# A decoder step of four recurrent branches: tile order, two groups of products on another engine, and re-timed side steps

## The chip, the cores and the metric

The kernel runs on one core of a Trainium2 chip. The metric is the time of one execution on the device in microseconds (us). A core has five engines that run side by side: PE (TensorE, matrix products), DVE (VectorE) and ACT (ScalarE) for elementwise work, POOL (GpSimd), and SP (SyncE), which here only issues DMA transfers.

## The reference

One layer of a hybrid recurrent decoder, on 2,096 positions (32 sample tokens of 8 sequences, 16 meta tokens, 2,048 prompt tokens), width 1,024:

```
u = x @ w_in                      # all branches' columns at once
A: xbc = silu(causal_conv(xbc));  chunked Mamba-2 scan, per-head RMS norm, * silu(z_a)
B: S5: diagonal complex state space, 16 groups of 16 channels, 64 states each;
   lb = exp(lam*dt), powers of lb, gelu, gated by a sigmoid product,       * silu(z_b)
C: qkv = silu(causal_conv(qkv)); q, k = l2norm(q), l2norm(k); gated DeltaNet in chunks:
   a triangular inverse per chunk, then a scan over chunks, RMS norm,      * silu(z_c)
D: HGRN2: f = lower bound + sigmoid, k = 1 - f; sum over q*k*decay, scan,  * silu(z_d)
out = concat(A, B, C, D) @ w_out
x   = layernorm(alpha * x + out)
```

The outputs are x and the seven final states, for the prompt and for each sample sequence.

## The kernel before, in words

After the input layer norm (phase1a), the positions are done in two halves (1,072 and 1,024). In each half `proj` (L585) runs 22 tiles of the input projection: one tile is 128 output columns times the half's positions, in 3 blocks (half 0: 384, 304, 384 columns) or 2 (half 1: 512), each of 24 matmuls into the PSUM tile pj. w and x are split in a high and a low part, hence three products of 8 each. After a block its `use` runs: for a tile with convolution (letters k, l, v, x in ORDER, L52) ScalarE copies pj to raw (L630 to L637), GpSimd makes cv = raw * w3 + b (L641), VectorE adds three shifted products (L643), ScalarE applies silu (L649 to L654), and SyncE stores it (L656: x to xbc_d, v to qkv_d); k and l then pass an l2 norm (`l2n`, L664). For f the `use` is two sigmoids and two scalings (L828 to L833); a, b, c, d are the gates z with silu (L815), q is D's query. The strings ORDER[0] and ORDER[1] give the order of the 22 tiles.

Everything else is "side work": Python generators ("jobs") that are resumed between the projection's matmuls. A job's `yield d` means: go on after d us of a clock that sums the nominal cost of the matmuls written so far (`_pe`, L115; `poll`, L140). Where the program needs a job to be finished, `drain` (L160) steps that clock on without projection matmuls between. TensorE runs its instructions in exactly the order in which the program was written so; the other engines' order comes from a scheduler. A changed number in a `yield` therefore moves that job's matmuls a few places along TensorE's order, and the scheduler's other queues follow.

The jobs that the change touches, and the names of their tiles:

- `small_loads` (L222): parameters, transposed on TensorE. `gates` (L484): A's and C's decays; te (L548) and g_rw (L565) come from cumulative sums, g_rw is transposed on TensorE and stored to rows_d.
- `b_setup` (L893): B's tables. `rot` (L977) builds cosT and sinT by doubling in rounds of products (L960 to L965, L999, L1000). L1061 and L1062 are 16 + 16 products of 128x144 into Pw and tw9, L1065 adds them (128x2304). L1074 to L1076 make four bs_wt, each transposed on TensorE. `b_main`, `b_tail`: B's scans.
- `c_pre` (L732): C's decay matrices; cdec is loaded from rows_d, masked on GpSimd (L727), exponentiated on ScalarE (L729), and multiplied into cma (L753, L755). `base_inv` (L763) inverts the small triangular blocks (acc) step by step on VectorE, `c_inv` and `c_chunk` use them.
- `d_group` (L1580): D. d_pr is the query-key product (L1596, buffers d_pra and d_prb), reduced per head by hsel on TensorE; Q blocks Qa, Qb (L1600) and running decays d_tota, d_totb follow on VectorE.
- At the first block of the tile with index LAST (L53), `last()` waits for the inverses, gives back the memory of the half, and in half 0 begins the next half's phase1a, in half 1 starts the heads of C and A (`c_head`, L1493) and their chunks. In the last stage, `out_chunk` (L1831) makes the 17 output chunks.

## Time and profile before

| what | value |
|---|---|
| three executions | 1395.56, 1398.35, 1405.71 us; median 1398.35 |
| the profiled execution | 1396.38 us, its span 1394.6 us, mean granted clock 0.945 |
| TensorE, matrix products | 1278.1 us busy, 92% |
| TensorE, weight loads | 1078.6 us, 77% |
| VectorE | 908.5 us, 65% |
| ScalarE | 573.4 us, 41% |
| GpSimd | 434.3 us, 31% |

The span runs from the first to the last instruction that the profiler recorded. The share of busy time is a mean over stages with different limits. An engine's idle time is put down to what released it ("releaser"). The granted clock is TensorE's, as a share of its full 2.4 GHz. In a row of the timeline stand the start in us, the duration in us, engine, line, operation, output and inputs, and in brackets the idle time before it with its releaser.

### The profile page before, as it was taken

The page shows a single profiled execution, that of the slowest core. Times are in us where ns is not written, and L with a number is a line of the kernel's source. Part 1 is how long each engine was busy: PE and PEld are TensorE (multiplying, and loading weights), DVE is VectorE, ACT ScalarE, POOL GpSimd, SP SyncE. Part 2 cuts the span into 40 slices and gives each one's busy share as a digit, 9 for nine tenths or more (in the row PEclk, how much of TensorE's full clock was granted, in tenths as well). Part 3 has the DMA queues.
Part 4 walks back from the last instruction along what each step waited for, and adds up shares of the span by engine and source line. Part 5 has one row for each costly group of instructions (what it writes and reads, how often), then busy time and mean ns, then how long its engine had stood idle before and what let it go on. Part 6 is the DMA issues. An engine that isn't in the chain of part 4 may idle for free.

```text
span 1394.6 us, 23821 instructions
## 1 busy us (share of the span) xinstructions
PE 1278.1 (92%) x8596; PEld 1078.6 (77%) x8596; DVE 908.5 (65%) x2269; ACT 573.4 (41%) x1089; POOL 434.3 (31%) x403
## 2 busy tenths in 40 slices
PE   6985996888999999999989889999997999999997
PEld 5885896877879998987767678778675677777886
DVE  8799623764698747766437598963347566756654
ACT  3234436366523443436375455353334333333211
POOL 4135111321211100102112222120115576677665
PEclk9998999998989999999999989999998999999999
DMA  8521243346424825313642734135639876776343
GB/s 220 175 84 42 55 149 91 90 133 196 127 76 143 236 77 189 110 46 96 184 135 72 249 112 118 51 105 147 173 99 284 202 216 188 204 191 201 118 121 107
DMA packets 259007, 195.80 MB, mean 140 GB/s; under 512 B 70949, under 2 KB 231927, under 8 KB 258872
## 3 DMA queue, kind: packets, MB, share of 16 engines
q1 hardware_dynamic: 258890, 194.28, 48.8%
q8 instruction: 68, 1.11, 0.4%
q14 instruction: 49, 0.40, 0.1%
HBM read 125.01 MB, written 64.31 MB: 136 GB/s over the span
## 4 chain that ended last, share of the span: by engine, by line
PE 49%; DVE 19%; DMA 14%; ACT 6%; POOL 5%; issue 4%; SPq 2%; POOLq 0%; DVEq 0%; ACTq 0%
PE pj L128 30%; PE pq L128 16%; DMA cdec<-rows_d 3%; PE pq L122 3%; DVE cv L643 2%; DMA f_R<-r_d 2%; DMA b<-b 1%; DMA bc<-nrm 1%; DVE w L582 1%; DMA a_L<-rows_d 1%; DVE Qa L1671 1%; DMA wr<-in_w_in_dram 1%; POOL xt L1870 1%; POOL xt L1871 1%; DVE d_ATa L1675 1%
## 5 line engine op out<-in xcount | busy, mean ns | idle before, releaser
L128 PE MATMUL pj<-xh,w 128*128 128x384 f32 (+2 forms) x1760 | 540.6, 375 | 7.9 <-ACT zs L832 3.1
L128 PEld LDWEIGHTS pj<-xh,w 128*128 128x128 f32 x1760 | 335.4, 197 | 52.9 <-issue 10.6
L128 PE MATMUL pj<-xl,w 128*128 128x384 f32 (+2 forms) x880 | 320.2, 364 | 0.0
L128 PEld LDWEIGHTS pj<-xl,w 128*128 128x128 f32 x880 | 174.2, 198 | 12.0 <-issue 0.2
L641 POOL TENSOR_SCALAR cv<-raw,par 128x384 f32<-128x384 f32 (+2 forms) x50 | 52.0, 1041 | 233.8 <-ACT raw L637 189.2
L128 PE MATMUL pj<-woh,o_mh 128*128 128x512 f32 (+2 forms) x280 | 116.1, 415 | 0.0
L128 PE MATMUL pj<-woh,o_ml 128*128 128x512 f32 (+2 forms) x280 | 109.0, 389 | 0.0
L128 PE MATMUL pj<-wol,o_mh 128*128 128x512 f32 (+2 forms) x280 | 108.9, 389 | 0.0
L643 DVE SCALAR_TENSOR_TENSOR cv<-raw,par,cv 128x384 f32<-128x384 f32 (+2 forms) x150 | 102.2, 683 | 9.7 <-POOL cv L641 8.8
L128 PE MATMUL pj<-w,xh 128*128 128x256 f32 (+3 forms) x544 | 105.9, 295 | 0.3 <-ACT xh L90 0.2
L128 PEld LDWEIGHTS pj<-w,xh 128*128 128x128 f32 (+1 forms) x544 | 85.1, 190 | 1.7 <-ACT xh L90 1.2
L128 PE MATMUL pj<-w,xl 128*128 128x256 f32 (+3 forms) x272 | 78.2, 291 | 1.5 <-DVE xl L90 1.5
L582 DVE TENSOR_TENSOR w<-wr,w 128x1024 fp32r<-128x1024 f32 x44 | 55.3, 1256 | 31.4 <-ACT w L581 31.3
L727 POOL TENSOR_TENSOR cdec<-cdec,negm 128x256 f32<-128x256 f32 x32 | 25.3, 791 | 159.1 <-DMA cdec<-rows_d 139.5
L128 PEld LDWEIGHTS pj<-woh,o_ml 128*128 128x128 f32 (+1 forms) x280 | 52.1, 186 | 12.7 <-issue 0.9
L128 PEld LDWEIGHTS pj<-woh,o_mh 128*128 128x128 f32 (+1 forms) x280 | 52.2, 187 | 10.9 <-issue 0.7
L128 PEld LDWEIGHTS pj<-wol,o_mh 128*128 128x128 f32 (+1 forms) x280 | 52.3, 187 | 8.2 <-issue 0.2
L310 POOL TENSOR_TENSOR lnrs<-lnve,mhalf 128x1 f32<-128x1 f32 (+1 forms) x34 | 23.9, 704 | 105.8 <-DVE lnve L90 60.9
L753 DVE SCALAR_TENSOR_TENSOR cma<-pq,nbeta,cdec 128x128 f32<-128x128 f32 (+1 forms) x68 | 23.0, 339 | 49.0 <-ACT cdec L729 33.1
L128 PEld LDWEIGHTS pj<-w,xl 128*128 128x128 f32 (+1 forms) x272 | 51.4, 191 | 2.0 <-DVE xl L90 1.9
L581 ACT CAST w<-wr 128x1024 fp32r<-128x1024 f32 x44 | 46.0, 1046 | 16.7 <-DMA wr<-in_w_in_dram 11.9
L1773 POOL TENSOR_TENSOR f_r<-f_r,mhalf 128x12 f32<-128x12 f32 x17 | 38.8, 2283 | 29.7 <-DVE f_r L1772 29.7
(570 smaller groups left out, 2574.8 us busy)
## 6 DMA issues: line engine op xcount, KB each, us to landing
wr<-in_w_in_dram SPq DMA_DIRECT2D x46, 512.0 KB
xt<-in_x_prompt_dram SPq DMA_DIRECT2D x16, 512.0 KB
xn_d<-xt SPq DMA_DIRECT2D x16, 512.0 KB
ma<-cma SPq DMA_DIRECT2D x64, 128.0 KB
xt<-xn_d SPq DMA_DIRECT2D x16, 512.0 KB
out_dram<-xt SPq DMA_DIRECT2D x15, 512.0 KB
f_R<-r_d SPq DMA_DIRECT2D x32, 192.0 KB
cdec<-rows_d SPq DMA_DIRECT2D x32, 128.0 KB
```

Source lines behind the costliest of these rows:

```text
L122: self._pe(self.PE.transpose(out, in_, self.ident[r, r]), 0.02 + n / 1200)
L128: self._pe(self.PE.matmul(out, lhsT, rhs, start=start, stop=stop, **kw), 0.01 + n * (1 if rhs.dtype == F32R else 4) / 2400)
L310: self.G.tensor_tensor(rs[:n], ve[:n], self.mhalf[:n, 0:1], ALU.pow)
L581: S.copy(w[:, :, 0], raw)
L582: V.tensor_tensor(w[:, :, 1], raw, w[:, :, 0].bitcast(F32), SUB)
L641: G.tensor_scalar(cv[:, 0:m], raw[:, 3:3 + m], w[3], b, op0=MUL, op1=ADD)
L643: V.scalar_tensor_tensor(cv[:, 0:m], raw[:, k:k + m], w[k], cv[:, 0:m], op0=MUL, op1=ADD)
L727: G.tensor_tensor(d[:n, :, :n], d[:n, :, :n], m[:n, None, :n].to_broadcast([n, nh, n]), ADD)
L753: V.scalar_tensor_tensor(ma[:n, 0, h, :n], pks[h][:n, 0, :n], self.nbeta[:n, t, 2 * p + h:2 * p + h + 1], dec[:n, h, :n], op0=MUL, op1=MUL)
L1671: V.tensor_tensor(qv, qv, tv[r, :, :, 0:1].to_broadcast([64, 2, nbt, s]), MUL)
L1675: V.copy_predicated(AV[:nn, :, :, 1, :], mk, pa[:nn])
L1773: G.tensor_tensor(r, r, self.mhalf[:, 0:12], ALU.pow)
```

## The change

ORDER[0] goes from "qkkqbbllxvffvxxxccadda" to "qkkqbbllxffvvxcxxcadad", ORDER[1] from "kkbbqqllffvvxxxxccadda" to "kkbbqqllffvxxaxvxccadd", and LAST from 17 and 17 to 21 and 17. The products of L1061 and L1062, the sum of L1065 and the product of L1596 move from GpSimd to VectorE. Some twenty `yield` numbers change. The number of matmuls stays. VectorE has 42 instructions more (33 of the set-up, 9 of L1596), GpSimd 42 fewer; ScalarE's table loads go from 84 to 74, by the order in which its activations stand. The diff, with one line of surroundings:

```diff
@@ -49,8 +49,8 @@
 KORD = [0, 1, 4, 5, 6, 7, 2, 3]
-ORDER = ["qkkqbbllxvffvxxxccadda", "kkbbqqllffvvxxxxccadda"]
-LAST = [17, 17]
+ORDER = ["qkkqbbllxffvvxcxxcadad", "kkbbqqllffvxxaxvxccadd"]
+LAST = [21, 17]
 HEAD = META + NS
@@ -222,7 +222,7 @@
         a, V = self.a, self.Vp
-        yield 2.3
+        yield 3.6
 
@@ -240,7 +240,7 @@
                 yield 4.2
-        yield 3.8
+        yield 2.9
         p = self.pt()
@@ -530,7 +530,7 @@
 
-        yield 19.0
+        yield 19.0 if o else 24.7
         pa = self.pt()
@@ -555,7 +555,7 @@
                             self.segmask[:, :, None].to_broadcast([48, NSEG, 8]), MUL)
-            yield 1.0
+            yield 0.0
             pc = self.pt()
@@ -566,7 +566,7 @@
             k = min(8, N - t0)
-            yield 2.1
+            yield 2.7 if o else 2.1
             pt = self.pt()
@@ -685,7 +685,7 @@
                                 op=ADD, axis=mybir.AxisListType.X)
-        yield 9.0 if half else 6.1
+        yield 9.0 if half else 7.2
         p = self.pt()
@@ -697,7 +697,7 @@
             V.tensor_scalar(rf, rf, scale, None, op0=MUL)
-        yield 4.5 if half else 7.8
+        yield 4.5 if half else 6.4
         pt = self.pt()
@@ -789,7 +789,7 @@
                 V.tensor_tensor(T[:npar, j + 1:B, 0:j + 1], T[:npar, j + 1:B, 0:j + 1], tv, ADD)
-                yield 0.0 + m * (j + 1) / 240
+                yield 0.4 + m * (j + 1) / 240
             G.tensor_copy(D[:npar], T[:npar].rearrange("p i c -> p c i"))
@@ -921,7 +921,7 @@
         self.exp_acc(tp, mag, lrd)
-        yield 2.3
+        yield 2.7
         V.tensor_tensor(ang, li, dt, MUL)
@@ -946,7 +946,7 @@
         S.activation(cs, r2, AF.Sin)
-        yield 0.7
+        yield 0.6
 
@@ -987,7 +987,7 @@
             while w <= 64:
-                yield 1.6
+                yield 1.9
                 for c in range(0, min(w, 65 - w), 16):
@@ -1023,7 +1023,7 @@
         V.tensor_tensor(ci, ci, den, MUL)
-        yield 2.1
+        yield 0.9
         V.tensor_scalar(b2[0:64], b2[0:64], -1.0, None, op0=MUL)
@@ -1044,7 +1044,7 @@
                 self.ld(cl[:, :, j], a[nm][0].rearrange("(h g) q n -> (g q) h n", h=2))
-            yield 1.0
+            yield 0.9
             p = self.pt()
@@ -1058,11 +1058,11 @@
             yb = Yc[:, g:g + 1, :].to_broadcast(s9)
-            G.tensor_tensor(self.Pw[:, g], xb, pr[:, :, g:g + 1].to_broadcast(s9), MUL)
-            G.tensor_tensor(tw9[:, g], yb, pi[:, :, g:g + 1].to_broadcast(s9), MUL)
+            V.tensor_tensor(self.Pw[:, g], xb, pr[:, :, g:g + 1].to_broadcast(s9), MUL)
+            V.tensor_tensor(tw9[:, g], yb, pi[:, :, g:g + 1].to_broadcast(s9), MUL)
             if g % 4 == 3:
                 yield 2.5
-        G.tensor_tensor(self.Pw, self.Pw, tw9, ADD)
+        V.tensor_tensor(self.Pw, self.Pw, tw9, ADD)
 
@@ -1125,7 +1125,7 @@
         for hq in range(2):
-            yield 0.9 if hq else 4.7
+            yield 1.2 if hq else 4.7
             p = self.pt()
@@ -1133,7 +1133,7 @@
         for gh in range(2):
-            yield 1.0 if gh else 2.0
+            yield 1.0 if gh else 2.4 if blk < 2 else 2.0
             p = self.pt()
@@ -1172,7 +1172,7 @@
                          p.rearrange("p (g i q) -> p g i q", g=4, i=8), AF.Gelu_apprx_tanh)
-            yield 3.5 if hq else 3.9
+            yield 3.0 if hq else 3.9
         y5 = tp.tile([128, 2, 64, 8], F32, name="b2")
@@ -1215,7 +1215,7 @@
         S.copy(U, p[:, 0:288].rearrange("p (g c) -> p g c", g=16))
-        yield 5.0
+        yield 4.4
         p = self.pt()
@@ -1263,7 +1263,7 @@
                          p[:10].rearrange("p (g i q) -> p g i q", g=4, i=8), AF.Gelu_apprx_tanh)
-            yield 2.6
+            yield 2.8
         yield 1.7
@@ -1390,7 +1390,7 @@
                         dap(self.tb_d, (((NT + t0 + c) * 4) * 4 + b) * 1024, [[32, 32], [4096, 4], [1, 32]]))
-        yield 27.2 if t0 == 1 else 8.0
+        yield 28.0 if t0 == 1 else 8.0
         kd, vb = [], []
@@ -1508,7 +1508,7 @@
         qe, ke = eqk[:, 0], eqk[:, 1]
-        yield 10.8
+        yield 10.0
         p = self.pt()
@@ -1593,12 +1593,12 @@
         pr = tp.tile([128, 2, 256], F32, name="d_pr" + sfx)
-        G.tensor_tensor(pr[:, :, :NTK], qf[:, 0:2, :NTK], kS[:, :, :NTK], MUL)
+        V.tensor_tensor(pr[:, :, :NTK], qf[:, 0:2, :NTK], kS[:, :, :NTK], MUL)
         Q = self.Qbd[sfx]
         for h in range(2):
             r = slice(64 * h, 64 * h + 64)
             V.tensor_tensor(Q[r, :, h, :NTK], qf[r, 0:2, :NTK], qf[r, 2:4, :NTK], MUL)
-        yield 13.6 if tail else 8.0
+        yield 13.6 if tail else 7.0 if t0c in (1, 9, 11) else 8.0
         p = self.pt()
@@ -1760,7 +1760,7 @@
                         axis=mybir.AxisListType.X)
-        yield 1.1
+        yield 1.3
         p = self.pt()
@@ -1825,7 +1825,7 @@
                 self.bo = self.bcast_row(op2, a["ln_b"], "o_bo")
-            yield 8.9
+            yield 10.6 if half else 6.8
             self.done.add(("wo", half))
```

How instructions move is shown at three places.

VectorE, from the tile te on (half 0, tile 1; te is what the transposed g_rw waits beside; cv is the convolution, bs_wt the first of three set-up tables that TensorE transposes behind it). Before:

```order
L548 TENSOR_TENSOR te<-g_tot,g_acum 128x72
L962 TENSOR_TENSOR bvr<-bvr,bm_1369 128x16
L643 SCALAR_TENSOR_TENSOR cv<-raw,par,cv 128x384
L964 TENSOR_TENSOR bs_l<-sinT,bur 128x256
L1074 TENSOR_TENSOR bs_wt<-bs_X,bpr 128x128 x4
L643 SCALAR_TENSOR_TENSOR cv<-raw,par,cv 128x328
L964 TENSOR_TENSOR bm_1369<-bui,bur 128x16
L552 TENSOR_TENSOR dtte<-sp_115,te 128x36
L573 COPY g_rs<-pq 128x128
L643 SCALAR_TENSOR_TENSOR cv<-raw,par,cv 128x384
L965 TENSOR_TENSOR sinT<-sinT,bs_l 128x16x16
L660 COPY cprev<-raw 128x3
```

and now:

```order
L548 TENSOR_TENSOR te<-g_tot,g_acum 128x72
L1000 COPY bui<-bvi 128x16
L960 TENSOR_TENSOR cosT<-cosT,bur 128x16x16
L960 TENSOR_TENSOR bvr<-bur 128x16
L961 TENSOR_TENSOR bs_l<-sinT,bui 128x256
L963 TENSOR_TENSOR sinT<-cosT,bui 128x16x16
L961 TENSOR_TENSOR bm_1362<-bui 128x16
L963 TENSOR_TENSOR bvi<-bur,bui 128x16
L552 TENSOR_TENSOR dtte<-sp_115,te 128x36
L962 TENSOR_TENSOR cosT<-cosT,bs_l 128x16x16
L1074 TENSOR_TENSOR bs_wt<-bs_X,bpr 128x128 x4
L962 TENSOR_TENSOR bvr<-bvr,bm_1362 128x16
```

Before, the addition L1076 into bs_wt is the next row, behind three convolution rows; now two rows of the rotation (L960 to L965) follow, then L1076, and no convolution row stands between.

ScalarE, in half 0 around tiles 10 to 12 (zs is f's sigmoid, cdec C's decay, ACT_TABLE_LOAD the switch between their tables). Before:

```order
L828 ACT_TABLE_LOAD
L828 ACTIVATE zs<-pj 128x384
L832 ACTIVATE zs<-pj 128x384
L829 ACTIVATE zs<-zs,lb,lb_606 128x384
L833 ACTIVATE zs<-zs,lb_606 128x384
L729 ACT_TABLE_LOAD
L729 ACTIVATE cdec<-cdec,nac 128x128 x4
L828 ACT_TABLE_LOAD
L828 ACTIVATE zs<-pj 128x384
L832 ACTIVATE zs<-pj 128x384
L581 CAST w_3553<-wr 128x8x128
L829 ACTIVATE zs<-zs,lb,lb_606 128x384
```

and now:

```order
L828 ACTIVATE zs<-pj 128x304
L832 ACTIVATE zs<-pj 128x304
L829 ACTIVATE zs<-zs,lb,lb_616 128x304
L833 ACTIVATE zs<-zs,lb_616 128x304
L729 ACT_TABLE_LOAD
L729 ACTIVATE cdec<-cdec,nac 128x128 x2
L1140 COPY b_3378<-pq 128x512
L729 ACTIVATE cdec<-cdec,nac 128x128 x2
L1140 COPY b_3378<-pq 128x512
L729 ACTIVATE cdec<-cdec,nac 128x128 x4
L828 ACT_TABLE_LOAD
L828 ACTIVATE zs<-pj 128x384
```

Before, sigmoid and decay alternate with a load each time; now the blocks of f above the first shown row share one load with it, and eight decay activations stand in one row before the next switch.

SyncE, in half 1 from the last convolved tile's stores on (xbc_d and qkv_d hold convolved x and v; c_qk, c_aq, ep and c_N are what `c_head` reads). Before:

```order
L1709 DMA od_d<-d_oya 128x2x128
L656 DMA xbc_d<-zs 128x512
L796 DMA tb_d<-acc 128x1024
L806 DMA z_d<-zs 128x512
L1709 DMA od_d<-d_oya 128x2x128
L796 DMA tb_d<-acc 128x1024
L1498 DMA c_qk<-qkv_d 128x6x48
L1500 DMA c_aq_9200<-ma_74 48x4x48
L1709 DMA od_d<-d_oyb 128x2x128
L1948 DMA S_9192<-in_state_gdn_dram 64x8x64 x4
L1505 DMA c_N_9202<-tb_d 16x4x16
L806 DMA z_d<-zs 128x512
```

and now:

```order
L580 DMA wr<-in_w_in_dram 128x8x128
L1967 DMA out_dram<-SD 64x64 x3
L865 DMA out_dram<-zs 3x128
L656 DMA xbc_d<-zs 128x512
L1293 DMA ep<-rows_d 64x4x48 x2
L1498 DMA c_qk<-qkv_d 128x6x48
L1948 DMA S_9192<-in_state_gdn_dram 64x8x64 x4
L1500 DMA c_aq_9200<-ma_74 48x4x48
L1505 DMA c_N_9202<-tb_d 16x4x16 x3
```

Before, the last xbc_d store stands well ahead of c_qk with gate and state transfers between; now the loads of ep, c_qk and c_aq stand directly behind it.

## Rows read from the trace of the kernel before

**Rows 1.** Page, part 1: busy us, share of span, instructions.

```profile
PE 1278.1 (92%) x8596; PEld 1078.6 (77%) x8596; DVE 908.5 (65%) x2269; ACT 573.4 (41%) x1089; POOL 434.3 (31%) x403
```

**Rows 2.** Stretch: length; busy PE, PEld, DVE, ACT, POOL (instructions); clock, DMA share, GB/s.

```profile
96.00:125.73 29.73, 19.22 (x103) 18.48 (x103) 29.67 (x103) 5.51 (x14) 22.42 (x37) 0.82 0.12 36
118.30:146.20 27.90, 12.15 (x62) 11.30 (x63) 25.96 (x96) 14.75 (x31) 4.99 (x5) 0.76 0.11 28
330.00:350.00 20.00, 13.90 (x89) 11.69 (x88) 11.23 (x23) 13.52 (x22) 4.33 (x6) 0.76 0.74 203
788.00:850.00 62.00, 55.37 (x298) 46.32 (x298) 50.45 (x120) 35.44 (x78) 15.17 (x18) 0.92 0.50 153
850.00:910.00 60.00, 55.09 (x314) 44.76 (x312) 58.92 (x137) 19.89 (x45) 9.25 (x9) 1.00 0.30 88
910.00:1049.00 139.00, 138.95 (x887) 106.86 (x888) 60.49 (x153) 54.96 (x109) 24.97 (x27) 0.94 0.49 133
```

**Rows 3.** Waits of PE from 95 to 150 us: total, times, longest.

```profile
PE pq L122 <- DVE bs_wt L1076: 8.1, 3, 6.0
PE pq L122 <- DVE te L548: 7.7, 1, 7.7
```

**Rows 4.** Timeline of DVE, 98 to 123 us.

```profile
98.92 0.16 DVE L961 TENSOR_TENSOR bm<-bui 128x16 f32<-128x16 f32 x1
...
104.70 0.43 DVE L961 TENSOR_TENSOR bm<-bui 128x16 f32<-128x16 f32 x1
...
114.55 5.06 DVE L1000 COPY bui<-bvi 128x16 f32<-128x16 f32 x1
...
119.85 0.16 DVE L960 TENSOR_TENSOR bvr<-bur 128x16 f32<-128x16 f32 x1
119.94 0.41 DVE L961 TENSOR_TENSOR bs_l<-sinT,bui 128x256 f32<-128x256 f32 x1
120.27 0.41 DVE L963 TENSOR_TENSOR sinT<-cosT,bui 128x256 f32<-128x256 f32 x1
```

**Rows 5.** Timeline of POOL, 95 to 130 us.

```profile
98.03 6.67 POOL L1061 TENSOR_TENSOR Pw<-bs_Xc,bpr 128x144 f32<-128x144 f32 x15
...
114.47 5.10 POOL L1065 TENSOR_TENSOR Pw<-Pw,bs_w 128x2304 f32<-128x2304 f32 x1
```

**Rows 6.** Waits of PE, 200 to 222 us.

```profile
PE pq L128 <- DVE cma L755: 6.7, 2, 4.5
```

**Rows 7.** Timeline of ACT, 326 to 336 us.

```profile
333.06 0.69 ACT L729 ACTIVATE cdec<-cdec,nac 128x128 f32<-128x128 f32 x2 [5.30 <-POOL cdec L727]
333.77 1.28 ACT L828 ACT_TABLE_LOAD   x1
```

**Rows 8.** Waits of PE, 325 to 350 us.

```profile
PE pj L128 <- ACT zs L832: 3.1, 1, 3.1
PE pq L128 <- DVE cma L755: 3.0, 2, 2.7
```

**Rows 9.** Timeline of all engines, 794 to 797 us.

```profile
794.34 1.39 DVE L1600 TENSOR_TENSOR Qa<-d_qfa 64x512 f32<-64x512 f32 x2 [0.36 <-DMA d_qfa<-qfk_d]
...
796.09 2.35 DVE L1600 TENSOR_TENSOR Qb<-d_qfb 64x512 f32<-64x512 f32 x2
...
796.54 1.36 POOL L1596 TENSOR_TENSOR d_pra<-d_qfa,d_ka 128x512 f32<-128x512 f32 x1 [20.10 <-DMA d_ka<-qfk_d]
```

**Rows 10.** Waits of PE, 790 to 910 us.

```profile
PE pq L128 <- DVE d_tota L1649: 2.8, 1, 2.8
...
PE pq L128 <- POOL d_pra L1596: 1.2, 1, 1.2
```

**Rows 11.** Timeline of SP, 915 to 960 us.

```profile
928.82 0.33 SPq L656 DMA_DIRECT2D xbc_d<-zs  x1
...
935.60 0.43 SPq L1498 DMA_DIRECT2D c_qk<-qkv_d  x1
```

**Rows 12.** Timeline of PE, 955 to 958 us.

```profile
956.72 0.60 PE L122 MATMUL pq<-ident,c_qk 128*48 128x128 f32 x4
```

## The prediction

> **What bounds the kernel now.** I read the page's first part first. TensorE is busy 92% of the span [rows 1], so the projection's matmuls are the bound, and time can be won where TensorE idles or runs at the lower clock. Every term below is idle time on TensorE, with what ended it. The profiled execution took 1396.38 us (its span of 1394.6 and 1.8 around it); the median of the three runs is 1398.35, 2.0 higher. The sum is made against 1396.4, and 2.0 is added at the end.
>
> Second, busy time by stretch [rows 2]. From 118.3 to 146.2 us TensorE works 12.15 of 27.90 us at a granted clock of 0.76 (a mix of the levels 2.4 and 1.2 GHz) while VectorE is full (25.96). From 330 to 350 it works 13.90 of 20.00, at 0.76. From 788 to 910 it misses 6.6 + 4.9 = 11.5 us, and VectorE is at 58.92 of 60.00 in the second half of that. From 910 to 1049 it misses nothing (138.95 of 139.00).
>
> Third, TensorE's waits in the first of these: 7.7 us once for VectorE's te (L548), and 8.1 us in three waits, the longest 6.0, for VectorE's bs_wt (L1076) [rows 3]: 15.8 in all.
>
> Fourth, why VectorE is late there. It never idles; it is slowed. The product bm<-bui of 128x16 takes 0.16 us at 98.92 and 0.43 at 104.70; the copy of L1000, no larger, takes 5.06 at 114.55 [rows 4]. GpSimd runs L1061 and L1062 in the first of these stretches and from 114.47 for 5.10 us the one 128x2304 sum of L1065 [rows 5]. The copy starts 0.08 us behind that sum and ends 0.04 after it: VectorE stood still for a whole GpSimd instruction. The small products lose 0.27 each beside instructions of 6.67 / 15 = 0.44.
>
> **The change, term by term.**
>
> *Set-up of B, L1061 to L1065 to VectorE.* Removed: 4.9 us of the copy (5.06 less the 0.16 of a 16-column instruction), and the stretching. Where GpSimd is quiet, VectorE starts the next instruction 0.09 us behind one of 16 columns and 0.33 behind one of 256 (119.85, 119.94, 120.27 [rows 4]), so about 0.08 + 0.001 a column. At that the 103 instructions that it runs from 96.0 to 125.73 [rows 2] need about 16.2 of these 29.7 us; 13.5 were lost. Added: 32 products of 144 columns at 0.22 are 7.0, and one sum of 2304 columns is 2.4: 9.4. So VectorE gains 13.5 - 9.4 = 4.1. The order moves more: two rotation rounds that stood ahead of te stand behind it, l2 transposes and reductions come ahead, and the five convolution instructions between te and the first bs_wt behind it are gone. I get te 3.4 us earlier and the three bs_wt 4 to 8 earlier; the waits become about 4.5, 0.8, 2.3 and 0.8, in all 8.4 where 15.8 stood, a gain of 7. Bounds: if only the block of 4.9 goes and no stretching, te comes 9.4 - 4.9 = 4.5 **later**; if all waits go, 15.8 are won. I take 6, near the worked value and under it, since convolution products (L641) still run on GpSimd there.
>
> *Half 0's l2n, c_pre and b_tail.* The drain at the sixth tile idles TensorE for 6.7 us behind cma [rows 6]. Six matmuls more are laid before it: about 1. Bounds 0 and 2.
>
> *ORDER of half 0, "vffv" to "ffvv" around tiles 9 to 12.* f tiles need the sigmoid on ScalarE, c_pre's decay the exponential, and each switch loads a table, 1.28 us; now ScalarE waits 5.30 for a decay operand, then loads, and only then copies zs [rows 7]. TensorE stands 3.1 behind zs and 3.0 behind cma [rows 8]. The changed order has 74 table loads instead of 84, five fewer in this stretch (17 for 22), but two f tiles still stand behind four decay activations each. ScalarE is busy only 13.52 of 20.00 [rows 2], so not all of 5 x 1.28 = 6.4 lies on the path. I take 3 of the 6.1 idle. Bounds: 6 won, or 3 lost if late operands hold both tiles.
>
> *D's product (L1596) to VectorE.* On GpSimd 1.36 us for 128x512; beside it VectorE's Qb pair needs 2.35 where Qa's needs 1.39 [rows 9]. On VectorE one takes 0.08 + 0.51 = 0.6. At 796 to 803 TensorE waits 1.2 for it and 2.8 for d_tota, behind the slowed instructions [rows 10]. Added 1.2, freed at least 0.96, and the product ends 0.8 earlier. The other seven lie beside matmuls without a wait that long. About 1; bounds 0 and 4.
>
> *ORDER of half 1 ("vvxxxxccadda" to "vxxaxvxccadd"), base_inv's 0.4 a step.* A tile without convolution now stands between x tiles, and one tile's convolution leaves the stretch where VectorE is at 58.92 of 60 for the one where it is at 60.49 of 139 [rows 2]. The inverse's steps are spread over 13 us more. Of the 7.5 idle left in 788 to 910 (11.5 less the 4.0 above) I take 2. Bounds: 6 won, 4 lost.
>
> *The rest* (small_loads, rot, b_main, b_tail, rms, c_inv, out_setup): steps move by 0.1 to 3 us between matmuls, some earlier, some later. I put 0, covered by the matmuls beside them; where a step's operand is late now, its whole delay shows: 3 either way. LAST 21 moves one drain, but the loads for the next half keep their place on SyncE's queue.
>
> Sum: 6 + 1 + 3 + 1 + 2 = 13. So 1396.4 - 13 = 1383.4, and with the 2.0, **1385 us**. I add no clock gain (rival 3).
>
> **A rule set against the rows.** The small products lose 0.27 us beside GpSimd instructions of 0.44 [rows 4, 5]; the copy lost the whole 4.9. The Trainium skill, "SBUF — State Buffer", section "Who interferes with whom", says that VectorE and GpSimd share one port pair as an exclusive lock, and that the one who comes second is fully blocked. The copy agrees; rival 2 is what it would make of the small ones.
>
> **Rivals.**
>
> *1. Only the set-up pays.* For it: the other stretches are held by operands that come late (the 5.30 wait), which the change leaves. 1396.4 - 7 + 2 = 1391; range 1390 to 1399. Chance 0.22.
>
> *2. Every GpSimd product blocks VectorE for its whole length.* Then 32 x 0.44 + 4.9 = 19.0 of the 29.7 were lost, not 13.5, VectorE's own need is 10.7, te comes at 96.0 + 10.7 + 9.4 = 116.1, before TensorE asks for it, and all 15.8 of waits go: 1396.4 - 15.8 - 7 + 2 = 1376; range 1372 to 1379. For it: the copy. Against: the spacings, which give 16.2. Chance 0.05. This is the lock of the Trainium skill's "SBUF — State Buffer", taken strictly.
>
> *3. The clock comes back too.* TensorE's 12.15 us at 0.76, 13.90 at 0.76 and 55.37 at 0.92 [rows 2] would be 2.9, 3.3 and 4.4 shorter at full clock, 10.6 in all. If shorter waits return two thirds of that, 1385 - 7 = 1378; range 1371 to 1381. For it: the lowest clocks stand beside the waits. Against: half the waits stay, and 910 to 1049 has 0.94 without any. Chance 0.17.
>
> *4. Slower: C's head waits.* Now the last xbc_d store is issued at 928.82, and c_qk is loaded from 935.60 for a step at 956.72 [rows 11, 12], 21 us ahead. After the change the last convolved tile is one tile (about 22 us) later, just before that step's job starts; the loads of ep, c_qk and c_N stand behind its last store, then at about 951, 5 us ahead of the step. Each us that VectorE lags there beyond some 2 is a wait of TensorE in a stretch that has no idle now. From 15 us of such a lag it eats the 13, and 25 give 1385 + 23 = 1408; range 1399 to 1412. VectorE being half idle past 910 speaks against it. Chance 0.08.
>
> *The forecast,* 1381 to 1390: 0.48.
>
> **Numbers.** About 1% (14.0 us, to 1384.4) is what a measurement of this kernel tells from no change. The forecast's range straddles it, with 0.22 of its 0.48 below; with rivals 2 and 3 that is 0.44 faster. Rival 1, the other 0.26 and 0.01 of rival 4 are the same: 0.49. Slower 0.07. The range of 8 in 10 leaves out the lowest of rival 3 and most of rival 4: 1372 to 1400.
>
> **What would show it.** Right: no GpSimd products at 97 to 119, no 16-column instruction over 0.2 there, waits behind te and bs_wt of 8 us instead of 15.8; fewer than 80 table loads; no wait behind L1596; VectorE under 55 of 60 before 910. Wrong: te later than 126; a zs wait of over 3 us; a wait at c_qk's or c_N's step; new waits past 1100, where I put nothing.

## The result, and the profile after

| | runs | median (us) | ratio to before, 95% interval |
|---|---|---|---|
| before, on the same chip | 4 | 1402.03 (1395.56 to 1415.68) | |
| after | 4 | 1387.27 (1385.89 to 1388.38) | 0.988 [0.984, 0.992] |
| after again, on another chip (before there: 1406.84) | 4 | 1389.70 | 0.990 [0.987, 0.992] |

The forecast was 1385. The profiled execution took 1386.24 us, with a span of 1384.5 and a mean granted clock of 0.951, against 1396.38, 1394.6 and 0.945. This is part 1 of the page after, the row that answers to [rows 1]:

```profile
PE 1273.9 (92%) x8596; PEld 1075.5 (78%) x8596; DVE 903.5 (65%) x2311; ACT 561.2 (41%) x1079; POOL 411.8 (30%) x361
```

The number of matmuls is the same. Span less PE's busy time is TensorE's idle time: 116.5 us before, 110.6 after. So of the 10.1 us between the two spans 5.9 are idle time and 4.2 are busy time: the same matmuls took less time at a higher mean clock. The forecast was 13 of idle time and none of the clock.

Busy time by stretch after (columns as in [rows 2]); the first window is the stage of the set-up, from the first matmul of tile 0 to that of tile 3, and took 69.7 us before:

```profile
86.30:151.60 65.30, 49.42 (x281) 44.97 (x281) 60.70 (x273) 27.06 (x57) 15.81 (x15) 0.87 0.16 47
109.70:142.00 32.30, 18.90 (x96) 17.47 (x95) 31.53 (x134) 12.18 (x33) 8.33 (x5) 0.75 0.09 24
320.00:342.00 22.00, 16.21 (x104) 14.07 (x103) 15.58 (x29) 14.01 (x25) 4.68 (x7) 0.84 0.50 142
781.00:841.00 60.00, 51.79 (x279) 42.73 (x280) 47.70 (x119) 32.62 (x73) 12.14 (x16) 0.89 0.54 161
841.00:900.00 59.00, 58.57 (x332) 48.84 (x332) 56.01 (x141) 22.55 (x50) 4.05 (x5) 1.00 0.28 84
900.00:1041.00 141.00, 141.00 (x895) 109.02 (x895) 68.84 (x158) 52.28 (x108) 29.82 (x30) 0.94 0.50 135
```

TensorE's idle time in the set-up stage went from 19.7 us to 65.30 - 49.42 = 15.9 (in the second profile of each kernel, of which more below, from 18.5 to 15.0). The window from 320 us is the one with the sigmoids: 5.79 idle of 22, against 6.10 of 20 [rows 2]. In the two windows of D's stage 8.2 and 0.4 are idle, 8.6 in all against 11.5, and VectorE works 56.01 of 59 in the second. From 900 to 1041, where the head of C stands, nothing is idle in this profile.

TensorE's waits in the set-up, after (columns as in [rows 3]: total, times, longest):

```profile
PE pq L128 <- DVE g_g L523: 8.7, 1, 8.7
PE pq L122 <- DVE bm L964: 3.0, 1, 3.0
PE pq L122 <- DVE bs_wt L1076: 1.7, 1, 1.7
...
```

The waits for te and most of those for bs_wt are gone. In their place stands one of 8.7 us for g_g, which ended no wait there in the profile before (1.8 in its second profile). VectorE's timeline shows why (start, duration):

```profile
97.84 0.99 DVE L1061 TENSOR_TENSOR Pw<-bs_Xc,bpr 128x144 f32<-128x144 f32 x4
...
104.75 1.21 DVE L582 TENSOR_TENSOR w<-wr,w 128x1024 fp32r<-128x1024 f32 x1
105.89 1.38 DVE L1062 TENSOR_TENSOR bs_w<-bs_Yc,bpi 128x144 f32<-128x144 f32 x6
...
108.06 0.42 DVE L964 TENSOR_TENSOR bm<-bui,bur 128x16 f32<-128x16 f32 x1
...
108.98 2.55 DVE L1065 TENSOR_TENSOR Pw<-Pw,bs_w 128x2304 f32<-128x2304 f32 x1
...
118.10 0.23 DVE L523 TENSOR_TENSOR g_g<-sp,g_ac 128x72 f32<-128x72 f32 x1
...
121.80 0.21 DVE L548 TENSOR_TENSOR te<-g_tot,g_acum 128x72 f32<-128x72 f32 x1
```

The 32 products start at 97.84. Where they stand in a row they follow each other by about 0.22 us, as the forecast had it, and the sum takes 2.55 (2.4 forecast). But they stand ahead of g_g, the first operand of the same chain that ends in te. That g_g was made at 112.27 before, and is made at 118.10 now. te comes at 121.80 (122.3 forecast, 125.73 before).

### The profile page after: what moved, and what is told of

Read it like the earlier page. It is cut to its first block, busy times and chain, and to the rows that moved or that the text cites. A ratio compares the mean times of both kernels' runs of the same rounds, so it can differ in the third digit from the quotient of the medians.

```text
span 1384.5 us, 23790 instructions
## 1 busy us (share of the span) xinstructions
PE 1273.9 (92%) x8596; PEld 1075.5 (78%) x8596; DVE 903.5 (65%) x2311; ACT 561.2 (41%) x1079; POOL 411.8 (30%) x361
## 4 chain that ended last, share of the span: by engine, by line
PE 43%; DVE 15%; DMA 9%; ACT 4%; issue 3%; POOL 3%; SPq 1%; POOLq 0%; DVEq 0%; ACTq 0%
PE pj L128 25%; PE pq L128 16%; PE pq L122 2%; DMA cdec<-rows_d 2%; DVE cv L643 1%; DMA b<-b 1%; DVE Qa L1671 1%; DVE d_ATa L1675 1%; DMA xt<-in_w_out_dram 1%; DMA f_R<-r_d 1%; DVE w L582 1%; DVE y L1794 1%; POOL f_R L1793 1%; DMA qfk_d<-zs 1%; DMA a_L<-rows_d 1%
## 5 line engine op out<-in xcount | busy, mean ns | idle before, releaser
L641 POOL TENSOR_SCALAR cv<-raw,par 128x384 f32<-128x384 f32 (+2 forms) x50 | 54.9, 1099 | 304.8 <-ACT raw L637 236.8
L128 PE MATMUL pj<-woh,o_mh 128*128 128x512 f32 (+2 forms) x280 | 116.1, 415 | 0.0
L128 PEld LDWEIGHTS pj<-w,xh 128*128 128x128 f32 (+1 forms) x544 | 86.2, 193 | 1.4 <-ACT xh L90 1.0
L582 DVE TENSOR_TENSOR w<-wr,w 128x1024 fp32r<-128x1024 f32 x44 | 54.1, 1229 | 32.9 <-ACT w L581 32.9
L128 PEld LDWEIGHTS pj<-woh,o_mh 128*128 128x128 f32 (+1 forms) x280 | 52.3, 187 | 11.3 <-issue 1.4
L815 ACT ACTIVATE zs<-pj 128x384 f32<-128x384 f32 (+2 forms) x40 | 20.7, 519 | 64.7 <-PE pj L128 55.9
```

The source lines that it names most:

```text
L128: self._pe(self.PE.matmul(out, lhsT, rhs, start=start, stop=stop, **kw), 0.01 + n * (1 if rhs.dtype == F32R else 4) / 2400)
L582: V.tensor_tensor(w[:, :, 1], raw, w[:, :, 0].bitcast(F32), SUB)
L641: G.tensor_scalar(cv[:, 0:m], raw[:, 3:3 + m], w[3], b, op0=MUL, op1=ADD)
L815: S.activation(z, p, AF.Silu)
```

## The experiments

The idle time of a profiled execution alone doesn't tell what a part is worth: with identical matmuls PE's busy time lay between 1273.9 and 1290.5 us in the fourteen profiles. So the table sets beside each ratio two means over the timed executions, each of which has its span and its mean granted clock: span x clock, and span x (1 - clock). The second is what the lower clock would cost if TensorE never idled at it; the two add up to the span.

| kernel | ratio [95%] | runs | span x clock | span x (1 - clock) |
|---|---|---|---|---|
| before, on the four chips of the experiments | | 59 | 1318.5 | 84.5 |
| after | 0.988 [0.984, 0.992] | 4 | 1317.3 | 68.2 |
| after again | 0.990 [0.987, 0.992] | 4 | 1314.3 | 73.9 |
| before again | 1.000 [0.997, 1.004] | 10 | 1320.1 | 83.1 |
| before + set-up on VectorE | 1.002 [0.999, 1.006] | 8 | 1320.7 | 87.7 |
| before + tile order | 1.005 [1.002, 1.009] | 6 | 1321.4 | 89.6 |
| before + step times | 1.012 [1.009, 1.015] | 4 | 1331.9 | 87.3 |
| after, set-up on GpSimd | 0.995 [0.993, 0.997] | 4 | 1320.5 | 76.9 |
| after, D's product on GpSimd | 0.995 [0.992, 0.997] | 6 | 1318.8 | 76.0 |
| after, products asked for later | 0.991 [0.988, 0.994] | 10 | 1316.9 | 75.0 |
| after, products behind te | 0.995 [0.992, 0.998] | 11 | 1320.0 | 74.6 |
| the same, rotation later too | 0.989 [0.986, 0.992] | 5 | 1316.6 | 69.6 |
| after, gates' step back to 19.0 | 0.991 [0.989, 0.994] | 5 | 1315.2 | 75.1 |
| the last two together | 0.991 [0.988, 0.994] | 6 | 1316.1 | 73.2 |

**The set-up alone.** The kernel before with the set-up's three lines on VectorE:

```diff
-            G.tensor_tensor(self.Pw[:, g], xb, pr[:, :, g:g + 1].to_broadcast(s9), MUL)
-            G.tensor_tensor(tw9[:, g], yb, pi[:, :, g:g + 1].to_broadcast(s9), MUL)
+            V.tensor_tensor(self.Pw[:, g], xb, pr[:, :, g:g + 1].to_broadcast(s9), MUL)
+            V.tensor_tensor(tw9[:, g], yb, pi[:, :, g:g + 1].to_broadcast(s9), MUL)
...
-        G.tensor_tensor(self.Pw, self.Pw, tw9, ADD)
+        V.tensor_tensor(self.Pw, self.Pw, tw9, ADD)
```

> The kernel before with one edit: the 32 products and the sum of B's set-up on VectorE. Theory (the gain of the set-up is the contention, and most of it turns into a new wait for g_g, since 9.4 us of products stand ahead of it on VectorE): the copy of L1000 at 0.16 us, te's wait gone, a wait of about 8 us behind g_g in its place, bs_wt's waits down from 8.1 to about 4; 2 to 4 us faster than before. Rival 1 (the freed time is all gained): 10 to 16 us faster. Rival 2 (VectorE only gets 9.4 us more work): 3 to 6 us slower.

It took 1410.94 us (ratio 1.002): no gain. Its waits in the set-up:

```profile
PE pq L128 <- DVE g_g L523: 7.9, 1, 7.9
PE pq L122 <- DVE bs_wt L1076: 5.7, 1, 5.7
```

13.6 us stand where 15.8 stood, or 14.5 in the other profile of the kernel before. The waits came much as the theory had them: the copy of L1000 takes 0.16 again, and the wait has moved from te up to g_g. So with the old steps the move is worth 1 to 2 us of waits, and nothing in the time.

**The order alone.**

```diff
-ORDER = ["qkkqbbllxvffvxxxccadda", "kkbbqqllffvvxxxxccadda"]
-LAST = [17, 17]
+ORDER = ["qkkqbbllxffvvxcxxcadad", "kkbbqqllffvxxaxvxccadd"]
+LAST = [21, 17]
```

> The kernel before with the two strings of ORDER and with LAST changed, all else as before. Theory (the order of tiles carries the larger part: a tile without convolution between two with one lets VectorE catch up, which shows in half 0 around 395 to 430 us and in half 1 from 840 to 900 us): 6 to 10 us faster, no half-clock stretch of 17 us near 405, under 2 us of waits from 840 to 900. Rival (the order pays only with its re-timed steps): within 3 us of before.

1411.77 us, ratio 1.005: slower, if anything, and not the 6 to 10 us faster of the theory. The wait for zs is shorter here (1.1 for 3.1), that for cma longer (4.4 for 3.0), and span x (1 - clock) is 89.6, where the kernel before has a mean of 86.2 on that chip.

**The step times alone.** All the yields of the change and nothing else, for example:

```diff
-        yield 19.0
+        yield 19.0 if o else 24.7
...
-                yield 1.6
+                yield 1.9
```

> The kernel before with all the changed step times (the yields) and nothing else. Theory (they give some 3 us back at the sixth tile's drain and lose as much in half 1 behind L1125): within 3 us of before, a wait for b (L1125) of about 3 us near 645. Rival (the re-timing carries the change): 6 us or more faster.

1420.81 us, ratio 1.012: slower by 1.2%. Two waits of TensorE stand out, in the set-up and at the sigmoids:

```profile
PE pq L122 <- DVE bs_wt L1076: 10.5, 3, 6.8
PE pq L128 <- DVE g_g L523: 8.6, 1, 8.6
```

```profile
PE pj L128 <- ACT zs L832: 10.0, 3, 4.2
```

The set-up's waits are 19.1 us (15.8 before), those for zs 10.0 (3.1). These 3.3 and 6.9 are most of what span x clock gained over the kernel before, 13.4. The step times cost by themselves; they are made for the other parts.

**The change without the set-up.** Lines L1061, L1062 and L1065 of the changed kernel back on GpSimd (the first diff reversed).

> The changed kernel with the set-up's products and sum back on GpSimd. Theory (set-up worth 2 to 4): 2 to 5 us slower than the changed kernel's 1387, with the copy of L1000 at about 5 us again and waits for te or bs_wt of 15 us. Rival 1 (set-up worth 10 or more): 1396 or more. Rival 2 (set-up worth nothing): 1386 to 1388.

1399.50 us, ratio 0.995, 10 to 12 us slower than the changed kernel on its two chips: rival 1's time, where the theory had 2 to 5. The waits in the set-up:

```profile
PE pq L122 <- DVE bs_wt L1076: 11.2, 3, 5.2
PE pq L128 <- DVE g_g L523: 4.1, 1, 4.1
PE pq L128 <- DVE g_gs L556: 3.9, 1, 3.9
```

They are 19.2 us, as much as with the step times alone; with the products on VectorE they are 13.4 (12.5 in the second profile). That completes a table of two by two: with the old steps the move takes 15.8 to 13.6, with the new ones (and the new order) 19.2 to 13.4.

The expectation had the copy of L1000 at 5 us again, but it takes 0.17 here. Another instruction is held, again for the length of GpSimd's sum:

```profile
113.60 5.12 DVE L962 TENSOR_TENSOR cosT<-cosT,bs_l 128x128 f32<-128x128 f32 x1
```

```profile
113.48 5.09 POOL L1065 TENSOR_TENSOR Pw<-Pw,bs_w 128x2304 f32<-128x2304 f32 x1
```

So the block belongs to the sum and not to the copy. In all five profiles with the sum on GpSimd one VectorE instruction between 85 and 160 us takes 5.0 to 5.1 us; in the nine with the sum on VectorE none there takes over 2.55. What the step times move is where it falls: behind g_gs (L556) in the kernel before, directly ahead of g_g with the step times alone (bvi, from 112.47; g_g comes at 117.39), between g_g and g_gs here. That fits the waits' other names in each kernel.

**The two kernels again**, unchanged, on the chip of the next two experiments.

> The kernel before itself, unchanged, for its spread. Theory (executions of one kernel differ by where the half clock falls, not by their waits): TensorE's waits over 0.4 us sum to within 2 us of the 103.8 of the first profile, and the span is 1211 us plus the waits plus half of the half-clock time, so about 175 us of half clock where the time is 1406. Rival (some transfer or wait differs): waits longer by 6 us or more. Ratio to itself 1.000, within 0.004.

> The changed kernel itself, unchanged, on the chip of the others. Theory: 1386 to 1389 again, ratio 0.985 to 0.990, spread under 5 us. Rival (its four executions were a favourable draw as the kernel before had in its first): 1395 or more, ratio over 0.993.

The kernel before took 1404.73 us and is itself (1.000). Its two profiles differ by 8.6 us of span, 4.6 of them idle (121.1 for 116.5) and 4.0 busy (1282.1 for 1278.1), so the expectation that this is not in the waits held for half of it: TensorE's waits over 0.4 us sum to 111.0, against 106.6 in the first profile by the same count. The changed kernel's second profile has 111.9 us idle and 1277.2 busy. Against the second of before that is 9.2 less idle and 4.9 less busy.

**The products later.** In the changed kernel the products are written behind the W1 tables, behind the same number of steps, so that g_g should not wait for them.

```diff
-        for g in range(16):
...
-            V.tensor_tensor(self.Pw[:, g], xb, pr[:, :, g:g + 1].to_broadcast(s9), MUL)
...
+            for g in range(4 * gq, 4 * gq + 4):
...
+                V.tensor_tensor(self.Pw[:, g], xb, pr[:, :, g:g + 1].to_broadcast(s9), MUL)
```

> The changed kernel, with the 32 products and the sum of the set-up still on VectorE but written behind the W1 tables instead of ahead of them, eight behind each quarter; the steps keep their places. Theory (in the changed kernel the products stand ahead of g_g, and TensorE waits 8.7 us for it): the wait for g_g under 2 us, the waits for g_g, te, bs_wt and bm together 4 to 8 where they are 13.4; 4 to 8 us faster than the changed kernel. Rival (VectorE is full from 95 to 142 us, and the wait only moves to the product of X and Pw behind L1088): within 2 us of the changed kernel.

1393.91 us, ratio 0.991. The edit did not do what it was made for: VectorE's order comes from the program's scheduler and not from the order of writing, the products and their sum still ran from 96.7 to 111.6 us, and the wait for g_g was 9.9. The run tells nothing of its question.

**D's product back on GpSimd.**

```diff
-        V.tensor_tensor(pr[:, :, :NTK], qf[:, 0:2, :NTK], kS[:, :, :NTK], MUL)
+        G.tensor_tensor(pr[:, :, :NTK], qf[:, 0:2, :NTK], kS[:, :, :NTK], MUL)
```

> The changed kernel with D's query-key product (L1596) back on GpSimd. Theory (it is worth about 1 us at 790 us and nothing elsewhere): 0 to 3 us slower than the changed kernel, a longer wait behind d_pra near 790. Rival (VectorE is the bound where D's groups run, so nine products of 0.6 on it cost): 2 to 5 us faster.

1397.30 us, ratio 0.995, against 0.990 for the changed kernel on the same chip. The product on VectorE is worth some 7 us, where 1 was forecast (the intervals of the two ratios just meet), but near it there is less to see:

```profile
PE pq L128 <- DVE d_sda L1608: 2.3, 1, 2.3
...
PE pq L128 <- POOL d_pra L1596: 1.1, 1, 1.1
```

These 3.4 us answer to the 2.9 for d_pra in the changed kernel. The stage of D has 10.4 us idle here and 8.6 (7.9) with the product on VectorE. Most of the rest stands where none of the nine products runs: between 700 and 755 us TensorE waits 10.8 for B's block (L1156, L1184), against 5.7 and 6.7 in the two profiles of the changed kernel. How the product leads to that is not shown.

**The products behind te**, now with an ordering edge that the scheduler must keep (the products written as above):

```diff
+                    self.tc.add_manual_dep(ins.ins, self.tei, mybir.DependencyInfo(
+                        mybir.DependencyClass.NoSync, mybir.DependencyReason.DATA), reason="order")
```

> The changed kernel with the set-up's products written behind the W1 tables (as in e7, where VectorE's order had come out unchanged) and now also held behind te by an ordering edge on VectorE, so that they do stand behind g_g and te. Theory (the order on VectorE makes the wait): g_g at about 108 us, its wait under 1 us, te's and bs_wt's together under 7, so 5 to 8 us faster than the changed kernel. Rival (VectorE is full from 95 to 140 us and everything there must be done before X times Pw, so the wait only moves): the waits from 95 to 150 us sum to 11 to 15 as before, time within 2 us of the changed kernel.

1394.38 us, ratio 0.995: it gains about half of what the changed kernel gains (0.988, 0.990). The profile is of the longest of the eleven executions (1405.10). In it te is there at 114.79, and there is no wait for g_g. But the wait came back one tile further on, for bs_wt:

```profile
PE pq L122 <- DVE bs_wt L1069: 14.8, 3, 5.4
```

```profile
114.79 0.21 DVE L548 TENSOR_TENSOR te<-g_tot,g_acum 128x72 f32<-128x72 f32 x1
...
121.67 0.67 DVE L1069 TENSOR_TENSOR bs_wt<-bs_wt,bs_wu 128x512 f32<-128x512 f32 x1
```

From te to the sum into the first bs_wt 6.9 us pass, with thirteen of the products and steps of the rotation between. VectorE does not rest once from 110 to 130 us (DVE 20.00 of 20.00):

```profile
110.00:130.00 20.00, 12.44 (x73) 11.52 (x71) 20.00 (x88) 9.41 (x20) 8.30 (x4) 0.91 0.13 38
```

So the rival was right about the waits: they are 14.8, in its range of 11 to 15. VectorE is full there, and this order only chose another operand to be late. It was not right about the time, which is 5 to 7 us over the changed kernel's, on another chip.

**And the rotation later.** As above, with the rounds of the rotation from w = 16 on behind the last bs_wt:

```diff
-                yield 1.9
+                yield 9.0 if w == 16 else 1.9
...
+                    if w >= 16:
+                        for ins in first:
+                            self.tc.add_manual_dep(ins.ins, self.wti, mybir.DependencyInfo(
+                                mybir.DependencyClass.NoSync, mybir.DependencyReason.DATA), reason="order")
```

> As the run before it, with the rotation's rounds of 256 columns (w of 16 and more) also held behind the last W1 table, whose consumers come later. Theory (VectorE's work that nobody waits for yet stands ahead of what TensorE waits for): 4 to 6 us of VectorE's work leave the stretch, the waits from 95 to 150 us come to 4 to 8, 6 to 10 us faster than the changed kernel. Rival 1 (the wait moves on to what needs the rotation, in B's blocks): waits of 4 us or more for cosT or sinT behind 150 us. Rival 2 (the clock decides): waits fall by 6 and the time by under 2.

1390.36 us, ratio 0.989, as the changed kernel. The waits are 13.7 us, where 14.8 stood and 4 to 8 were expected, in two places:

```profile
PE pq L122 <- DVE bs_wt L1074: 10.7, 3, 5.2
PE pq L122 <- DVE b_tm L1247: 3.0, 1, 3.0
```

**The gates' step of half 1 back to 19.0.** The changed kernel has a new wait of TensorE in half 1:

```profile
PE pq L122 <- DVE b L1125: 3.1, 1, 3.1
```

The cause stands on SyncE's queue and on VectorE (release in brackets):

```profile
638.53 0.90 SPq L725 DMA_DIRECT2D cdec<-rows_d  x2
639.48 1.24 SPq L1122 DMA_DIRECT2D b<-u_d  x2
```

```profile
646.93 0.69 DVE L1125 COPY b<-b 128x1024 f32<-128x1024 f32 x1 [4.83 <-DMA b<-u_d]
```

The load of b is issued at 639.48, behind two loads of cdec at 638.53, and is there 7.4 us later (7.5 in the second profile); in the kernel before, where the loads of cdec stand 8 us ahead of it, the same took 5.0 (649.04 to 654.06). Both come after the store of the gates' rows, which the 24.7 us step puts off.

```diff
-        yield 19.0 if o else 24.7
+        yield 19.0
```

> The changed kernel with the gates' first step in half 1 back at 19.0 from 24.7. Theory (the later step puts the loads of cdec straight ahead of those of B's block, which then land 7.4 us after their issue where it was 5.0, and TensorE waits 3.1 us for L1125 near 645): that wait under 1 us, 3 to 4 us faster than the changed kernel. Rival (the load is slow for another reason): the wait stays at 3 us, no change.

```profile
630.01 1.44 SPq L725 DMA_DIRECT2D cdec<-rows_d  x2
...
638.80 1.24 SPq L1122 DMA_DIRECT2D b<-u_d  x2
```

cdec is loaded 8.5 us earlier, b stands 8.8 us behind it and is there after 5.1, and there is no wait between 630 and 670 us: the theory of this wait holds. Yet the time was 1392.89 us, ratio 0.991, and the idle time 113.0 for 110.6 and 111.9. A wait of 4.1 us for c_N (L1422, in C's chunks) near 990 us stands in its profile; but such a wait comes and goes between the two profiles of the changed kernel itself (none and 2.2), so it can't be put down to the edit.

**The last two together.**

> The changed kernel with the products and the late rotation rounds held behind te and the last W1 table (as in e10) and the gates' first step in half 1 at 19.0 (as in e11). Theory (waits add up): the waits of the set-up at 10 to 11 us and none for L1125 near 645, together 5 us less than the changed kernel has; ratio to the kernel before 0.984 to 0.988. Rival (what waits give back at this size is lost in where the half clock falls): 0.988 to 0.992, not to be told from the changed kernel.

1392.28 us, ratio 0.991, not told apart from the changed kernel, as the rival had it. The waits of the set-up are 11.8 us and there is none for L1125 near 645, so 4 to 5 us of waits went there and the time did not follow. None of these versions is faster than the changed kernel.

## Why the forecast was right, and where it was not

**The sum: right in size, not in kind.** 13 us were forecast against a measured 14.8 between the medians of one chip, and the time lay 2 us from the forecast. That it came so close is in part luck: the sum was set against a median of 1398.35, which a fourth execution raised to 1402.03, and terms that were too high and a clock gain that was put at nothing made up for each other. Two pairs of profiles give 5.9 and 9.2 us of idle time, and 4.2 and 4.9 of busy time. In the timed executions span x (1 - clock) falls from 84.5 to 68.2 and 73.9, and span x clock only from 1318.5 to 1317.3 and 1314.3. As an estimate, over the fourteen profiles PE's busy time rises by 0.73 us with each us of span x (1 - clock) (correlation 0.94); at the means of the 59 executions before and the 8 after that makes 10 us of busy time and 6 of idle time. So "I add no clock gain" is the term that failed most; rival 3 held part of the truth, beside a smaller gain in idle time than the sum had.

The signs that the prediction named say the same. The GpSimd products are gone and there are 74 table loads. But the waits behind g_g, bm and bs_wt are 13.4 and not 8, some 16-column instructions still take over 0.2 us there (0.42 at 108.06), there is a wait behind L1596 (2.9), VectorE works 56.01 us of 59 before 900, and a wait for zs of over 3 us, named as a sign of being wrong, came (3.6; 5.0 in the second profile).

**Where the clock came back.** The rows show the same stretch of the program, from the first matmul of tile 3 to that of tile 14 in half 0, the same 1395 matmuls or so in each kernel (columns as in [rows 2]). Before and before again,

```profile
155.72:388.08 232.36, 203.47 (x1396) 184.76 (x1396) 126.20 (x309) 118.06 (x209) 47.22 (x43) 0.92 0.47 128
```

```profile
156.12:391.51 235.39, 205.97 (x1396) 186.99 (x1396) 125.61 (x312) 118.43 (x209) 48.11 (x43) 0.90 0.46 127
```

with the order alone, with the step times alone,

```profile
156.20:392.47 236.27, 207.95 (x1395) 188.67 (x1395) 123.55 (x306) 113.53 (x205) 50.13 (x43) 0.89 0.46 126
```

```profile
157.26:397.79 240.53, 207.29 (x1396) 187.34 (x1395) 129.91 (x326) 115.07 (x206) 46.98 (x43) 0.90 0.45 124
```

and in the changed kernel without the set-up, and in the changed kernel itself:

```profile
158.20:386.20 228.00, 199.24 (x1395) 180.51 (x1394) 123.19 (x312) 111.09 (x203) 46.20 (x42) 0.93 0.48 130
```

```profile
151.79:378.96 227.17, 200.17 (x1395) 181.03 (x1395) 123.12 (x312) 110.97 (x203) 45.19 (x42) 0.94 0.48 131
```

The clock is 0.89 to 0.92 in the first four and 0.93 to 0.94 in the last two. Over all fourteen profiles it is 0.892 to 0.919 in the five that lack the order or the step times, and 0.925 to 0.940 in the nine that have both, where this stretch is 227 to 230 us long instead of 232 to 241. TensorE's idle time in it hardly differs (28.9 us before, 28.8 without the set-up, 27.0 in the changed kernel); its busy time falls by 3.3 us in the first pair of profiles and 5.4 in the second, which is about all the busy time that the change saves (4.2 and 4.9). So the clock's part of the gain lies mostly here, and it takes order and step times together. Rival 3 looked for it at the three longest stalls; the set-up's lowest stretch in fact stayed at 0.75.

Parts that are slower by 0.5% and 1.2% alone give 0.5% less time together (0.995, with one of the two groups of products moved). Order and step times with neither group moved were not run, and why the lower clock falls where it does is not shown.

**B's set-up: 6 forecast; 2.4 us of waits and 3.8 of idle time found between the two kernels.** The price of the products and of the sum was right, as was te. The step that failed is "the waits become about 4.5, 0.8, 2.3 and 0.8": 13.4 came, because the sum looked at te alone and not at g_g, which stands ahead of it on the same engine and was put off by 5.8 us. (With the products held behind te the wait for g_g is gone.) The move by itself is worth about 6 in the changed kernel, 19.2 to 13.4; but 3.4 of these only make good what the new step times cost in this place (15.8 to 19.2), which was put at 0.

**The lock.** What rival 2 forecast did not come: 13.4 us of waits are left where it had none, and te came at 121.80, not at 116.1. One GpSimd instruction is left beside the products:

```profile
105.69 2.78 POOL L641 TENSOR_SCALAR cv<-raw,par 128x328 f32<-128x328 f32 x1 [7.44 <-ACT raw L632]
```

It runs from 105.69 to 108.47, 2.78 us, where the same form takes 0.64 at 224.00 in the same trace: here it was GpSimd that lost time. It came while VectorE's L582 (from 104.75) was running. The six products from 105.89 on take 0.23 each and lose nothing; only the bm of 128x16 at 108.06 takes 0.42 and ends at 108.48, with the GpSimd instruction. The Trainium skill, "SBUF — State Buffer", section "Who interferes with whom", has a VectorE instruction with two inputs contend with a GpSimd instruction that reads, and the one that comes later wait. The trace agrees: GpSimd came second here and was held, as VectorE's two-input cosT (113.60) came second beside the sum (113.48) in the kernel without the set-up, and took 5.12.

**The drain: 1 forecast.** The wait for cma fell from 6.7 to 4.1 us, by more than the stated bound of 2. But the second profile of the kernel before has 3.6 there, and the second of the changed kernel 4.1, so no gain of this term is shown.

**The order of half 0: 3 forecast, about 0 found in idle time.** TensorE's wait for zs rose from 3.1:

```profile
PE pj L128 <- ACT zs L832: 5.4, 2, 3.6
```

and ScalarE shows the reason:

```profile
330.22 0.69 ACT L729 ACTIVATE cdec<-cdec,nac 128x128 f32<-128x128 f32 x2 [3.53 <-POOL cdec L727]
330.93 1.28 ACT L828 ACT_TABLE_LOAD   x1
332.23 0.49 ACT L828 ACTIVATE zs<-pj 128x384 f32<-128x384 f32 x1
```

The decay at 330.22 still comes 3.5 us late from GpSimd, with its table load ahead of the sigmoid's, as rival 1 said ("operands that come late, which the change leaves"). There are 74 table loads for 84, as forecast, and ten fewer of them took no wait away. The 3.0 behind cma went; 5.79 of 22 us are idle for 6.10 of 20. What came was the clock: 0.84 for 0.76 in these two windows.

**D's product and the order of half 1: 1 and 2 forecast, 2.9 found together** (11.5 to 8.6; 7.9 in the second profile). The order's part of it is shown: from the first matmul of tile 10 to that of tile 17 in half 1, TensorE's idle time is 11.5 and 11.3 us in the two profiles of the kernel before, 8.7 with the order alone, 11.4 with the step times alone, and 8.6 and 6.5 in the changed kernel. D's stretch on VectorE and on TensorE:

```profile
790.63 1.38 DVE L1600 TENSOR_TENSOR Qb<-d_qfb 64x512 f32<-64x512 f32 x2
...
792.36 0.68 DVE L1596 TENSOR_TENSOR d_pra<-d_qfa,d_ka 128x512 f32<-128x512 f32 x1
```

```profile
PE pq L128 <- DVE d_pra L1596: 2.9, 1, 2.9
...
```

The product takes 0.68 where it took 1.36 and no longer slows Qb (1.38 for 2.35), but it stands behind both Q blocks now, and TensorE waits 2.9 for it (1.3 in the second profile) in place of 1.2; the 2.8 for d_tota are gone. "No wait behind L1596" was wrong, and VectorE is at 56.01 of 59, not under 55 of 60 (51.87 of 59 in the second profile). That this product alone is worth some 7 us in the time is not explained by its stage.

**The rest: 0 forecast.** Not nothing: the step times alone cost 13 us of span x clock, and in the changed kernel the late load of b costs a new wait of 3.1. (All waits for L1125 together are 11.6 us, against 12.2 before: others of them got shorter.)

**The head of C.** Rival 4 did not come: the loads behind the last store were no wait in a stretch without idle time. In the first profile only 0.4 us of a wait ended there from 900 to 1041. In the second there are 3.7, none of them at the head's step; c_N and c_vb are here tiles of C's chunks:

```profile
PE pq L122 <- ACT c_N L1422: 2.2, 1, 2.2
PE pq L128 <- ACT c_vb L1404: 1.1, 1, 1.1
PE pq L128 <- ACT Qa L1640: 0.4, 1, 0.4
```

Three of the variants have 3.4 to 4.1 us for c_N in that place, the others none. In the kernel before, neither profile has one: so a little of this stretch is at times lost after the change, and the forecast had nothing for it.

## What to carry to other kernels

When work moves to an engine that is full in that stretch, follow all the operands it makes for the engine that waits, the first as well as the last: here te came 3.9 us earlier and g_g 5.8 later. Don't price step times and order apart from each other: each alone was slower or no faster here, and only together did they pay. And where one profile is set against another, split the span into idle and busy time first: here 4.2 of 10.1 us, and 4.9 of 14.1 in the second pair, were the same matmuls taking less time. To see where, set stretches of the same matmuls against each other.

## What the runs showed of the hardware that was not expected

- The same 8596 matmuls took 1273.9 to 1290.5 us of busy time in fourteen profiles, at mean granted clocks of 0.951 to 0.936. The kernel before alone ran at 0.934 to 0.949 in 59 executions.
- Taking a wait away did not shorten the time by it: the 3.1 us at L1125, gone by one edit, gave nothing measurable.
- Beside GpSimd's 128x2304 sum of 5.0 to 5.1 us, VectorE's next instruction took as long, in five profiles of five: a 128x16 copy, a 128x16 product or a 128x128 subtraction. The other way round, a GpSimd instruction that takes 0.64 us elsewhere took 2.78 beside VectorE's products.
- A 128x2304 sum takes 2.55 us on VectorE and 5.10 on GpSimd; a 128x512 product 0.68 and 1.36.
